# A two-layer feed-forward on one Trainium2 core: three quarters of the second matrix product by Strassen's seven block products

## The chip, the core and the metric

One core of one Trainium2 chip (trn2) runs the whole program. The metric is the device time of one execution in microseconds (us). Engines are named as in the profile: PE is TensorE's matmul stream, PEld its weight loads, DVE is VectorE, ACT is ScalarE, POOL is GpSimd, SP is SyncE, whose queue issues the weight transfers. Each engine runs its own instructions in a fixed order, written when the program is compiled, and the engines meet through semaphores.

## The reference, cut to what matters

The model is three blocks on 512 tokens of width 1024, all in float32. The change is in the feed-forward that ends each of the two layers of the second block:

```python
def squared_relu_mlp(n, w_up, w_down):          # n: 512 x 1024
    return jnp.square(jax.nn.relu(n @ w_up)) @ w_down   # w_up 1024 x 4096, w_down 4096 x 1024

for layer in range(DEPTH_2):                    # DEPTH_2 = 2
    n = rmsnorm_2(h, g_mix[layer])
    h = h + mixer(n, ...)                       # sparse attention + gated linear attention, then stick-breaking attention
    h = h + squared_relu_mlp(rmsnorm_2(h, g_ffn[layer]), w_up[layer], w_down[layer])
```

## The kernel before, in words

Activations stand feature-major: `x` is a list of eight tiles of 128 features by 512 tokens. A float32 product is made of three matmuls in the type fp32r: each operand is split into a rounded `hi` and a rest `lo`, and hi·hi, hi·lo and lo·hi are added up in PSUM. ACT writes `hi` (L148 for activations, L170 for weights), DVE writes `lo` (L149, L171).

- `proj_fm` (feature-major) loads 256 columns of a weight matrix in one transfer of 1 MB into `raw` (two buffers), splits them in two halves of 128 columns into `whi` and `wlo` (three buffers each, L170 and L171), and calls `fm_tile` for each half: 8 blocks of the contraction times three matmuls (L246 to L248), 24 matmuls with 512 moving columns and 128x128 weights, into one PSUM bank of the tag `mm` (four banks). Then `evac` takes the bank.
- `proj_tok` (token-major) does the same with the activations as weights and 512 columns of the weight matrix moving (L282 to L284), four banks at a time.
- `first()` raises the priority of what is traced in it, so that the compiler's scheduler places splits and evictions early in their engines' queues. Within that the scheduler orders instructions by when their inputs and buffers are ready.
- `mlp_up` (L1098) makes one quarter of the hidden features, 1024 of 4096: eight `fm_tile`s, each taken by DVE (`ha`, L1107: relu times the norm's scale), squared on ACT (L1108) and split again (L148, L149).
- The feed-forward of layer 0 loops over four quarters `g`: `mlp_up`, then `proj_fm` over the 1024 rows of `w_down0` that belong to the quarter; each of its eight tiles is added to `x` by DVE (`add_to`, L1075), the last quarter's by `residual` (L1066), which also splits for the next layer.
- The feed-forward of layer 1 does the same, but the second product is token-major: in quarter 0 the eight tiles of `x` are transposed by PE (L331) and copied by ACT (L1240) to `xo`, and every quarter adds to `xo` on DVE (L1245); the last quarter sends `xo` out.
- Every slot of 128x512 float32 comes from a tag with a fixed number of buffers (`SLOTS`): `s` 39, `o` 8, `go` 6, `isc` 3, `att` 4, `Ss` 4, `pTs` 2, `g` 4, `sq` 2. `kz` are the keys of an early attention, padded with zeros by POOL (L400).

Of the kernel before, what the change touches and what calls it, by code (L numbers as in the profile page):

```python
# [8 lines left out]
F32 = mybir.dt.float32  # L9
# [25 lines left out]

SLOTS = {"s": 39, "x": 8, "o": 8, "att": 4, "isc": 3, "go": 6, "Ss": 4, "pTs": 2, "g": 4, "sq": 2}

FILL = 480  # L40
BANKS = {"mm": 4, "S0": 1, "S1": 1, "pT": 1, "acc": 1}


def body(tc, A, out, dbg=None):
# [3 lines left out]
    with ExitStack() as es:  # L48
# [26 lines left out]
        def first():  # L75

            return tc.high_priority(3000)
# [28 lines left out]
            o, w = CV[name]  # L106
            return vec[:, o:o + w]

        ident = cp.tile([P, P], F32, name="ident")
# [77 lines left out]
        def later(f):  # L187
            pending.append(f)
# [35 lines left out]
        def drain(gen):  # L224
            for _ in gen:
                pass
# [27 lines left out]
        def proj_fm(W, r0, c0, ncols, xs, evac):  # L254


            kd = len(xs)
            w = 1024 // kd
            for ch in range(0, ncols, 2 * w):
                cw = min(2 * w, ncols - ch)  # L260
                raw = load_raw(kd, cw, (0, W[r0:r0 + kd * P, c0 + ch:c0 + ch + cw]))
                for hf in range(0, cw, w):
                    hi, lo = split_w(raw[:, :, hf:hf + w], w)
                    for mt in range(0, w, P):
                        fm_tile(hi, lo, mt, xs, evac, (ch + hf + mt) // P)
                        yield
# [158 lines left out]
        with tc.issue_after(box["v"].ins):  # L425
            gab = cp.tile([P, 3 * P], F32, name="gab")
            nc.scalar.dma_start(gab, A["gab"])
            ropeA = cp.tile([P, NT, 2, 32], F32, name="ropeA")
            nc.scalar.dma_start(ropeA, A["ropeA"])
            ropeI = cp.tile([P, NT, 2, 16], F32, name="ropeI")  # L430
# [12 lines left out]
            NRB = rb.shape[1]  # L443
            bias = []
            for h2 in range(4):
                rv = slot("biasr", tag="g")
                for j in range(2):
                    h = 2 * h2 + j
                    nc.scalar.dma_start(rv[:, j * 256:(j + 1) * 256],
                                        bass.AP(tensor=rb.tensor, offset=rb.offset + h * NRB, ap=[[1, P], [1, 256]]))  # L450
                b = slot("bias", tag="go")
                DVE.tensor_copy(heads(b, 2), heads(rv, 2)[:, :, ::-1])
                for j in range(2):
                    DVE.memset(b[0:64, j * 256 + 192:(j + 1) * 256], NEG)
                    bias.append(b[:, j * 256:(j + 1) * 256])
# [290 lines left out]
        drain(proj_fm(W, 0, 2376, 256, nx, ev_kb))  # L746


        n0 = cp.tile([P, P], F32, name="negm0")
        POOL.memset(n0, 0.0)  # L750
        POOL.memset(n0[0:64, 64:128], NEG)
        negm = [n0]
# [345 lines left out]
        dump("x3", x)  # L1098


        def mlp_up(Wu, g, nxs, rbc):
            hid = [None] * KD

            def ev(i, ps):
                def f():
                    a = slot("ha", tag="g")
                    DVE.scalar_tensor_tensor(a, ps, 0.0, box[rbc], op0=ALU.max, op1=ALU.mult)  # L1107
                    ACT.activation(a, a, AF.Square)  # L1108
                    hid[i] = split(a, tag="o" if i < 4 else "s")
                if rbc in box:  # L1110
                    f()
                else:
                    later(f)

            drain(proj_fm(Wu, 0, g * 1024, 1024, nxs, ev))
            return hid

        nx4 = [None] * KD
        T4 = cp.tile([P, NT], F32, name="T4")
        t4sq = cp.tile([P, NT], F32, name="t4sq")  # L1120
        for g in range(4):
            hid = mlp_up(A["w_up0"], g, nx3, "t3b")
            if g == 3:
                ss4 = SumSq()
            drain(proj_fm(A["w_down0"], g * 1024, 0, 1024, hid,
                          add_to(x) if g < 3 else residual(x, ss4, "gm1", nx4, lambda: (
                              scale_of(ss4, T4)(), DVE.tensor_tensor(t4sq, T4, T4, op=ALU.mult)))))
        dump("x4", x)


# [98 lines left out]


        xo = []
        for g in range(4):
            hid = mlp_up(A["w_up1"], g, nx5, "t5b")
            if g == 0:
                for tt in range(NT):
                    row = []
                    for hf in range(2):
                        ps = transposed([(j, blk(x[hf * 4 + j], tt)) for j in range(4)])
                        t_ = slot("xo", tag="go" if hf else "att")
                        ACT.activation(t_, ps, AF.Copy)  # L1240
                        row.append(t_)
                    xo.append(row)
            for hf in range(2):
                def ev_o(tt, ps, hf=hf, g=g):
                    DVE.tensor_tensor(xo[tt][hf], ps, xo[tt][hf], op=ALU.add)  # L1245
                    if g == 3:
                        nc.sync.dma_start(out[tt * P:(tt + 1) * P, hf * 512:(hf + 1) * 512], xo[tt][hf])

                drain(proj_tok(A["w_down1"], g * 1024, hf * 512, hid, ev_o))


def host_arrays(inp):
# [53 lines left out]
```

## Time and profile before

| | |
|---|---|
| three runs | 1654.59, 1658.58, 1658.85 us; median 1658.58 us |
| the profiled execution | 1655.4 us, of which the span from first to last instruction is 1653.7 us |
| mean granted TensorE clock | 0.99 of full speed |
| matmuls | 7576, each with its own weight load |
| the two feed-forwards | 16 stages of 1024x1024 weights by 512 tokens, 43.5 us each: 696 us |
| transfers | 146 MB, 88 GB/s over the span |

How it is read: an engine's busy time is the union of its instructions. Matmuls are pipelined, so that one lasts about 390 ns from start to end while the next starts much earlier; the pace of PE is the distance between starts, not the duration of one. "Idle before" is the time that an engine stood still ahead of an instruction, with what released it behind the arrow.

### The profile page before, as it was taken

To read this page: it belongs to the slowest core of one execution; us is meant where nothing else is said; L and a number is where in the kernel's file an instruction comes from. 1 tells how busy PE (TensorE), PEld (TensorE's weight loads), DVE (VectorE), ACT (ScalarE), POOL (GpSimd) and SP (SyncE) were. 2 spreads that over 40 slices of the span, in tenths; PEclk is the share of its full clock that TensorE was granted. 3 is DMA by queue.
4 is the path that set the end of the run, shared out by engine and by line. 5 is a ranking of instruction groups with operands and counts; after the bars stand their busy time and mean duration, and the time that the engine had idled before them with its cause. 6 is when DMAs were issued, how large, how long until landed. Compare 5 with 4: busy or idle time off the path is not lost.

```text
span 1653.7 us, 19122 instructions
## 1 busy us (share of the span) xinstructions
PE 1620.5 (98%) x7576; PEld 1331.8 (81%) x7576; DVE 847.7 (51%) x1463; ACT 653.3 (40%) x1012; POOL 208.8 (13%) x295
## 2 busy tenths in 40 slices
PE   9999999999898889999999999999999999999999
PEld 7887888888687768888888888888888788888887
DVE  5546443444668885654343444444557734444342
ACT  6444333235544445443232323344554532323231
POOL 3100000003412641210000000211212200000000
PEclk9999999999999999999999999999999999999999
DMA  6421123223212111133323232222211323332222
GB/s 203 148 76 52 52 85 118 89 98 109 94 60 77 52 52 52 52 102 102 100 82 99 102 102 100 80 100 77 77 52 52 102 77 102 102 102 85 94 102 77
DMA packets 123065, 146.25 MB, mean 88 GB/s; under 512 B 4048, under 2 KB 96864, under 8 KB 122976
## 3 DMA queue, kind: packets, MB, share of 16 engines
q1 hardware_dynamic: 116704, 141.11, 25.9%
q10 hardware_dynamic: 6272, 3.92, 0.9%
q8 instruction: 59, 0.97, 0.2%
q14 instruction: 30, 0.25, 0.0%
HBM read 142.92 MB, written 2.10 MB: 88 GB/s over the span
## 4 chain that ended last, share of the span: by engine, by line
PE 91%; DVE 4%; POOL 2%; ACT 1%; issue 1%; DMA 0%; POOLq 0%; DVEq 0%
PE fm L246 19%; PE fm L248 19%; PE fm L247 19%; PE tk L282 8%; PE tk L283 8%; PE tk L284 8%; PE tr L331 3%; PE oc L1201 1%; PE S L1177 1%; PE S L469 1%; PE pa L493 1%; DVE wlo L171 1%; DVE isc L786 1%; DVE m L785 1%; PE gr L887 1%
## 5 line engine op out<-in xcount | busy, mean ns | idle before, releaser
L246 PE MATMUL fm<-hi,whi 128*128 128x512 f32 x1416 | 559.2, 395 | 0.0
L247 PE MATMUL fm<-lo,whi 128*128 128x512 f32 x1416 | 552.5, 390 | 0.8 <-DVE lo L152 0.8
L248 PE MATMUL fm<-hi,wlo 128*128 128x512 f32 x1416 | 552.8, 390 | 0.0
L170 ACT ACTIVATE whi<-raw 128x1024 fp32r<-128x1024 f32 (+1 forms) x262 | 276.9, 1057 | 691.7 <-PE fm L247 460.5
L171 DVE TENSOR_TENSOR wlo<-raw,whi 128x1024 fp32r<-128x1024 f32 (+1 forms) x262 | 328.3, 1254 | 276.8 <-ACT whi L170 276.0
L247 PEld LDWEIGHTS fm<-lo,whi 128*128 128x128 f32 x1416 | 266.4, 188 | 55.7 <-DVE lo L152 2.0
L248 PEld LDWEIGHTS fm<-hi,wlo 128*128 128x128 f32 x1416 | 266.0, 188 | 55.7
L246 PEld LDWEIGHTS fm<-hi,whi 128*128 128x128 f32 x1416 | 266.1, 188 | 53.4 <-issue 0.5
L282 PE MATMUL tk<-whi,hi 128*128 128x512 f32 x664 | 270.5, 407 | 0.7 <-ACT va L795 0.6
L283 PE MATMUL tk<-wlo,hi 128*128 128x512 f32 x664 | 262.1, 395 | 0.0
L284 PE MATMUL tk<-whi,lo 128*128 128x512 f32 x664 | 261.6, 394 | 0.0
L284 PEld LDWEIGHTS tk<-whi,lo 128*128 128x128 f32 x664 | 125.8, 189 | 26.6
L282 PEld LDWEIGHTS tk<-whi,hi 128*128 128x128 f32 x664 | 126.4, 190 | 24.8 <-ACT va L795 1.0
L283 PEld LDWEIGHTS tk<-wlo,hi 128*128 128x128 f32 x664 | 126.2, 190 | 23.5 <-issue 0.4
L308 POOL TENSOR_TENSOR ssq<-ssq,sq 128x512 f32<-128x512 f32 x25 | 38.6, 1553 | 567.1 <-ACT sq L306 566.8
L1075 DVE TENSOR_TENSOR xT<-fm,xT 128x512 f32<-128x512 f32 x48 | 33.1, 690 | 87.4 <-PE fm L248 87.3
L1107 DVE SCALAR_TENSOR_TENSOR ha<-fm,t3b 128x512 f32<-128x512 f32 x32 | 22.0, 691 | 80.0 <-PE fm L248 80.0
L1107 DVE SCALAR_TENSOR_TENSOR ha<-fm,t5b 128x512 f32<-128x512 f32 x32 | 22.0, 691 | 79.4 <-PE fm L248 79.4
L149 DVE TENSOR_TENSOR lo<-ha,hi 128x512 fp32r<-128x512 f32 x64 | 44.3, 692 | 3.0 <-ACT hi L148 3.0
L148 ACT ACTIVATE hi<-ha 128x512 fp32r<-128x512 f32 x64 | 40.5, 633 | 2.0
L1108 ACT ACTIVATE ha<-ha 128x512 f32<-128x512 f32 x64 | 39.6, 618 | 2.8 <-DVE ha L1107 2.8
L1190 DVE TENSOR_TENSOR_SCAN R<-sgn,zero 128x128 f32<-128x128 f32 (+3 forms) x32 | 27.0, 843 | 21.1 <-POOL sgn L1184 21.1
(308 smaller groups left out, 1371.7 us busy)
## 6 DMA issues: line engine op xcount, KB each, us to landing
raw<-in_w_up SPq DMA_DIRECT2D x32, 1024.0 KB, 5.1
raw<-in_w_down SPq DMA_DIRECT2D x32, 1024.0 KB, 5.0
raw<-in_w_in SPq DMA_DIRECT2D x22, 1024.0 KB, 5.1
raw<-in_w_in_ab SPq DMA_DIRECT2D x14, 1024.0 KB, 4.8
raw<-in_w_in_c SPq DMA_DIRECT2D x12, 1024.0 KB, 5.0
raw<-in_w_out SPq DMA_DIRECT2D x4, 1024.0 KB, 4.7
raw<-in_w_out_ab SPq DMA_DIRECT2D x4, 1024.0 KB, 4.8
raw<-in_w_out_c SPq DMA_DIRECT2D x4, 1024.0 KB, 4.8
```

The costliest lines, as they stand in the source:

```text
L148: ACT.activation(hi[:, cols], src[:, cols], AF.Copy)
L149: DVE.tensor_tensor(lo[:, cols], src[:, cols], hi[:, cols].bitcast(F32), op=ALU.subtract)
L170: ACT.activation(hi[:, ks, :], raw[:, ks, :], AF.Copy)
L171: DVE.tensor_tensor(lo[:, ks, :], raw[:, ks, :], hi[:, ks, :].bitcast(F32), op=ALU.subtract)
L246: PE.matmul(ps, wh, xh, start=k == 0, stop=False)
L247: PE.matmul(ps, wh, xl, start=False, stop=False)
L248: last = PE.matmul(ps, wl, xh, start=False, stop=k == kd - 1)
L282: PE.matmul(ps, xh, hi[:, j, :], start=k == 0, stop=False)
L283: PE.matmul(ps, xh, lo[:, j, :], start=False, stop=False)
L284: last = PE.matmul(ps, xl, hi[:, j, :], start=False, stop=k == kd - 1)
L331: PE.transpose(ps[:, j * P:(j + 1) * P], s_, ident)
L1107: DVE.scalar_tensor_tensor(a, ps, 0.0, box[rbc], op0=ALU.max, op1=ALU.mult)
```

## The change

In both layers the quarters 0, 1 and 2 of the second product go by Strassen's scheme in its form with seven products and shared sums. A pair of output tiles (256 features, `mp` 0 to 3) and a pair of contraction blocks form 2x2 blocks of 128x128 weights; the tokens are halved, so that the activations form 2x2 blocks of 128x256. Seven block products take the place of eight, each over four pairs of contraction blocks and three fp32r terms: 84 matmuls with 256 moving columns for a pair of output tiles, where 48 with 512 columns stood.

- `weight_forms` makes, from one `raw` of 1024x256, the split pieces A11 and A12 (one split of 1024 elements a row), and S1, S2, A22, S4 and S3 (four sums on DVE and five splits of 512 elements a row). A11/A12 and S1/S2 go into two of the three `whi`/`wlo` buffers, the other three into `isc` (hi) and `att` (lo).
- `forms` makes the pieces of two hidden tiles: four half sums on DVE, one half split (B11), three whole splits.
- `down_pair` runs the seven products into four banks, two products in each. Products 1 and 5, and 6 and 4, are kept in `E` for all three quarters (in quarter 0 by ACT, then added to by DVE); the others are added to `x` by DVE at once. `settle` adds `E` to `x` after the third quarter, seven DVE instructions for a pair of tiles.
- `mlp` orders the work: the first 256 columns of the next quarter's up stage now run ahead of the current quarter's down stage. Quarter 3 stays as it was. The transposes of `x` in layer 1 move from quarter 0 to the end of quarter 3's up stage.
- Slots: `s` 38, `go` 8; `kz` moves into the tag `x`; `ident`, `ropeI` and `n0` move into the room of a fill tile that shrinks by as much.

```diff
-SLOTS = {"s": 39, "x": 8, "o": 8, "att": 4, "isc": 3, "go": 6, "Ss": 4, "pTs": 2, "g": 4, "sq": 2}
-FILL = 480
+SLOTS = {"s": 38, "x": 8, "o": 8, "att": 4, "isc": 3, "go": 8, "Ss": 4, "pTs": 2, "g": 4, "sq": 2}
+FILL = 96
...
-                t_ = kz[2 * i + j] = slot("kz")
+                t_ = kz[2 * i + j] = slot("kz", tag="x")
...
+        def forms(q, b1, b2, res):
+            tA, tB = slot("tA", tag="pTs"), slot("tB", tag="pTs")
+            DVE.tensor_tensor(half(tB, 0), half(b1, 0), half(b1, 1), op=ALU.subtract)
+            DVE.tensor_tensor(half(tA, 0), half(b2, 1), half(tB, 0), op=ALU.add)
+            DVE.tensor_tensor(half(tB, 1), half(b2, 0), half(tA, 0), op=ALU.subtract)
+            DVE.tensor_tensor(half(tA, 1), half(b1, 1), half(b2, 1), op=ALU.subtract)
+            if q % 2 == 0:
+                res["B11"] = slot("hi", F32R), slot("lo", F32R)
+            h_, l_ = (half(t_, q % 2) for t_ in res["B11"])
+            ACT.activation(h_, half(b1, 0), AF.Copy)
+            DVE.tensor_tensor(l_, half(b1, 0), h_.bitcast(F32), op=ALU.subtract)
+            out = {"B11": (h_, l_)}
+            for (n1, n2), (src, tag) in {("T1", "T4"): (tB, "s"), ("T2", "T3"): (tA, "s"),
+                                         ("B21", "B22"): (b2, "o")}.items():
+                sp_ = split(src, tag=tag)
...
+        def weight_forms(raw):
+            r = raw.rearrange("p (j a) (b c) -> p j a b c", a=2, b=2)
+            a11, a12, a21, a22 = (r[:, :, a, b, :] for b in range(2) for a in range(2))
...
+            def put(src, hi, lo):
+                ACT.activation(hi, src, AF.Copy)
+                DVE.tensor_tensor(lo, src, hi.bitcast(F32), op=ALU.subtract)
+            with first():
...
+                put(raw[:, :, 0:P], hi, lo)
...
+                S = {n_: tile4(slot("ws", tag="Ss")) for n_ in ("S1", "S2", "S4", "S3")}
...
+                DVE.tensor_tensor(S["S1"], a21, a22, op=ALU.add)
+                DVE.tensor_tensor(S["S2"], S["S1"], a11, op=ALU.add)
+                for i, n_ in enumerate(("S1", "S2")):
+                    put(S[n_], hi2[:, i], lo2[:, i])
...
+                DVE.tensor_tensor(S["S4"], S["S2"], a12, op=ALU.add)
+                DVE.tensor_tensor(S["S3"], a11, a21, op=ALU.add)
+                for n_, src in (("A22", a22), ("S4", S["S4"]), ("S3", S["S3"])):
+                    h_, l_ = tile4(slot("wh", F32R, "isc")), tile4(slot("wl", F32R, "att"))
+                    put(src, h_, l_)
...
+        def down_pair(Wd, g, mp, F, x, E):
+            raw = load_raw(KD, 2 * P, (0, Wd[g * 1024:(g + 1) * 1024, mp * 2 * P:(mp + 1) * 2 * P]))
+            w = weight_forms(raw)
+            banks = [psum("sw") for _ in range(4)]
+            plan = (("A11", "B11"), ("S1", "T1"), ("S2", "T2"), ("A22", "T4"), ("A12", "B21"), ("S4", "B22"), ("S3", "T3"))
+            for n, (wf, xf) in enumerate(plan):
+                ps = banks[n // 2]
+                for j in range(4):
...
+                    PE.matmul(half(ps, n % 2), wh, xh, start=j == 0, stop=False)
+                    PE.matmul(half(ps, n % 2), wh, xl, start=False, stop=False)
+                    last = PE.matmul(half(ps, n % 2), wl, xh, start=False, stop=j == 3)
...
+                if n in (1, 3):
+                    if g == 0:
+                        E[mp][i] = slot("e", tag="go")
+                        ACT.activation(E[mp][i], ps, AF.Copy)
+                    else:
+                        DVE.tensor_tensor(E[mp][i], ps, E[mp][i], op=ALU.add)
+                elif n == 5:
+                    DVE.tensor_tensor(xa, ps, xa, op=ALU.add)
+                elif n == 6:
+                    DVE.tensor_tensor(heads(xb, 2), half(ps, 0)[:, None, :].to_broadcast([P, 2, H]), heads(xb, 2), op=ALU.add)
...
+            for g in range(4):
+                e_ = ev(g)
+                if g == 0:
+                    drain(proj_fm(Wu, 0, 0, 1024, nxs, e_))
+                else:
+                    if g < 3:
+                        forms(0, has.pop((g, 0)), has.pop((g, 1)), F)
+                    else:
+                        for mp in range(4):
+                            settle(mp, x, E)
+                    drain(proj_fm(Wu, 0, g * 1024 + 256, 768, nxs, lambda i, ps: e_(i + 2, ps)))
+                if g < 3:
+                    nxt = ev(g + 1)
+                    drain(proj_fm(Wu, 0, (g + 1) * 1024, 256, nxs, nxt))
+                    for mp in range(4):
+                        down_pair(Wd, g, mp, F, x, E)
+            return hid
...
-        for g in range(4):
-            hid = mlp_up(A["w_up1"], g, nx5, "t5b")
-            if g == 0:
-                for tt in range(NT):
...
+        hid = mlp(A["w_up1"], A["w_down1"], nx5, "t5b", x)
+        for tt in range(NT):
```

## Rows read from the trace of the kernel before

**Rows 1.** The page's first part: busy us, share of the span, instructions

```profile
PE 1620.5 (98%) x7576; PEld 1331.8 (81%) x7576; DVE 847.7 (51%) x1463; ACT 653.3 (40%) x1012; POOL 208.8 (13%) x295
```

**Rows 2.** The page's chain that ended last, shares of the span

```profile
PE 91%; DVE 4%; POOL 2%; ACT 1%; issue 1%; DMA 0%; POOLq 0%; DVEq 0%
```

**Rows 3.** Windows by stage: length, busy us of PE, PEld, DVE, ACT, POOL

```profile
804.38:847.90 43.52, 43.52 (x193) 36.04 (x192) 19.91 (x24) 16.59 (x23) 0.00 (x0) 1.00 0.31 99
847.90:891.42 43.52, 43.52 (x193) 36.04 (x192) 15.98 (x18) 9.65 (x11) 0.00 (x0) 1.00 0.30 94
...
1519.38:1562.90 43.52, 43.52 (x193) 36.04 (x192) 15.92 (x17) 9.42 (x10) 0.00 (x0) 1.00 0.30 94
```

**Rows 4.** Groups by shape, 715 to 1070 us: busy, mean ns, idle before

```profile
L246 PE MATMUL fm<-hi,whi 128*128 128x512 f32 x513 | 199.8, 389 | 0.0
...
L247 PEld LDWEIGHTS fm<-lo,whi 128*128 128x128 f32 x513 | 96.3, 188 | 20.1
```

**Rows 5.** PE's timeline at 475 us: start us, duration us

```profile
475.04 0.28 PE L157 MATMUL is<-hi,hi 128*128 128x256 f32 x1
475.16 0.28 PE L158 MATMUL is<-lo,hi 128*128 128x256 f32 x1
475.27 0.28 PE L159 MATMUL is<-hi,lo 128*128 128x256 f32 x1
475.39 0.40 PE L282 MATMUL tk<-whi,hi 128*128 128x512 f32 x1
475.63 0.40 PE L283 MATMUL tk<-wlo,hi 128*128 128x512 f32 x1
475.87 0.39 PE L284 MATMUL tk<-whi,lo 128*128 128x512 f32 x1
476.09 0.28 PE L157 MATMUL is<-hi,hi 128*128 128x256 f32 x1
```

**Rows 6.** The same view, eight matmuls of one column

```profile
1301.67 1.05 PE L315 MATMUL st<-ones,ssq 128*128 128x1 f32 x8
```

**Rows 7.** Groups by shape, DVE, whole span

```profile
L171 DVE TENSOR_TENSOR wlo<-raw,whi 128x1024 fp32r<-128x1024 f32 x260 | 327.0, 1258 | 276.5 <-ACT whi L170 275.8
L149 DVE TENSOR_TENSOR lo<-ha,hi 128x512 fp32r<-128x512 f32 x64 | 44.3, 692 | 3.0 <-ACT hi L148 3.0
L1075 DVE TENSOR_TENSOR xT<-fm,xT 128x512 f32<-128x512 f32 x48 | 33.1, 690 | 87.4 <-PE fm L248 87.3
...
L1192 DVE TENSOR_TENSOR sgp<-sgp,R 128x256 f32<-128x256 f32 x8 | 3.4, 424 | 0.9
```

**Rows 8.** DVE's timeline from 1519 us: start us, duration us

```profile
1519.38 0.69 DVE L1107 SCALAR_TENSOR_TENSOR ha<-fm,t5b 128x512 f32<-128x512 f32 x1 [2.69 <-PE fm L248]
1520.25 1.23 DVE L171 TENSOR_TENSOR wlo<-raw,whi 128x1024 fp32r<-128x1024 f32 x1 [0.18 <-ACT whi L170]
1521.44 0.69 DVE L149 TENSOR_TENSOR lo<-ha,hi 128x512 fp32r<-128x512 f32 x1
...
1539.10 2.73 DVE L1245 TENSOR_TENSOR xo<-tk,xo 128x512 f32<-128x512 f32 x4 [1.08 <-PE tk L284]
```

**Rows 9.** Groups by shape, ACT, whole span

```profile
L170 ACT ACTIVATE whi<-raw 128x1024 fp32r<-128x1024 f32 x260 | 275.7, 1060 | 691.3 <-PE fm L247 460.5 <-PE tk L284 186.5 <-issue 39.4
L148 ACT ACTIVATE hi<-ha 128x512 fp32r<-128x512 f32 x64 | 40.5, 633 | 2.0
...
L341 ACT ACTIVATE pTs<-tr 128x256 f32<-128x256 f32 x16 | 6.1, 383 | 8.3 <-PE tr L331 8.3
...
L1240 ACT ACTIVATE xo<-tr 128x512 f32<-128x512 f32 x8 | 4.7, 592 | 3.8 <-PE tr L331 3.8
```

**Rows 10.** DMA issues: KB each, median us to landing

```profile
raw<-in_w_down SPq DMA_DIRECT2D x32, 1024.0 KB, 5.0
```

**Rows 11.** Groups by shape, PE, whole span: transposes

```profile
L331 PE MATMUL tr<-ident,xT 128*128 128x128 f32 x32 | 4.9, 276 | 0.0
```

**Rows 12.** Groups by shape, POOL, whole span

```profile
L400 POOL MEMSET kz<- 64x512 f32 x8 | 4.2, 521 | 0.4
```

More of the change, by code (lines that the diff above doesn't have):

```diff
@@ L1098, in body @@
         dump("x3", x)
-        def mlp_up(Wu, g, nxs, rbc):
-            hid = [None] * KD
[L1104 to L1111, printed above, removed]
-                else:
-                    later(f)
-            drain(proj_fm(Wu, 0, g * 1024, 1024, nxs, ev))
+        H = T // 2
@@ new lines, in half, with relu_sq, ready @@
+        def half(t_, j):
+            return t_[:, j * H:(j + 1) * H]
+        def relu_sq(ps, rbc, tag):
+            a = slot("ha", tag=tag)
+            DVE.scalar_tensor_tensor(a, ps, 0.0, box[rbc], op0=ALU.max, op1=ALU.mult)
+            ACT.activation(a, a, AF.Square)
+            return a
+        def ready(rbc, f):
+            if rbc in box:
+                f()
+            else:
+                later(f)
+        def forms(q, b1, b2, res):
[13 more added lines that the diff above has]
+                sp_ = split(src, tag=tag)
+                for j, n_ in enumerate((n1, n2)):
+                    out[n_] = tuple(half(t_, j) for t_ in sp_)
+            res[q] = out
@@ new lines, in weight_forms, with tile4 @@
+        def weight_forms(raw):
+            r = raw.rearrange("p (j a) (b c) -> p j a b c", a=2, b=2)
+            a11, a12, a21, a22 = (r[:, :, a, b, :] for b in range(2) for a in range(2))
+            res = {}
+            def tile4(t_):
+                return t_.rearrange("p (j c) -> p j c", j=4)
+            def put(src, hi, lo):
+                ACT.activation(hi, src, AF.Copy)
+                DVE.tensor_tensor(lo, src, hi.bitcast(F32), op=ALU.subtract)
+            with first():
+                hi = wp.tile([P, 8, P], F32R, tag="whi", bufs=3, name=uid("whi"))
+                lo = wp.tile([P, 8, P], F32R, tag="wlo", bufs=3, name=uid("wlo"))
+                put(raw[:, :, 0:P], hi, lo)
+                for a, n_ in enumerate(("A11", "A12")):
+                    res[n_] = [(hi[:, 2 * j + a, :], lo[:, 2 * j + a, :]) for j in range(4)]
+                S = {n_: tile4(slot("ws", tag="Ss")) for n_ in ("S1", "S2", "S4", "S3")}
+                hi2 = wp.tile([P, 2, 4, P], F32R, tag="whi", bufs=3, name=uid("whi"))
+                lo2 = wp.tile([P, 2, 4, P], F32R, tag="wlo", bufs=3, name=uid("wlo"))
+                DVE.tensor_tensor(S["S1"], a21, a22, op=ALU.add)
+                DVE.tensor_tensor(S["S2"], S["S1"], a11, op=ALU.add)
+                for i, n_ in enumerate(("S1", "S2")):
+                    put(S[n_], hi2[:, i], lo2[:, i])
+                    res[n_] = [(hi2[:, i, j, :], lo2[:, i, j, :]) for j in range(4)]
+                DVE.tensor_tensor(S["S4"], S["S2"], a12, op=ALU.add)
[3 more added lines that the diff above has]
+                    put(src, h_, l_)
+                    res[n_] = [(h_[:, j, :], l_[:, j, :]) for j in range(4)]
+            return res
@@ new lines, in settle, with both @@
+        def settle(mp, x, E):
+            e15, e64 = E[mp]
+            xa, xb = x[2 * mp], x[2 * mp + 1]
+            def both(t_):
+                return t_[:, None, :].to_broadcast([P, 2, H])
+            DVE.tensor_tensor(heads(xa, 2), heads(xa, 2), both(half(e15, 0)), op=ALU.add)
+            DVE.tensor_tensor(half(xa, 1), half(xa, 1), half(e64, 0), op=ALU.subtract)
+            DVE.tensor_tensor(half(xa, 1), half(xa, 1), half(e15, 1), op=ALU.add)
+            DVE.tensor_tensor(half(e64, 0), half(e64, 0), half(e15, 0), op=ALU.subtract)
+            DVE.tensor_tensor(heads(xb, 2), heads(xb, 2), both(half(e64, 0)), op=ALU.add)
+            DVE.tensor_tensor(half(xb, 0), half(xb, 0), half(e64, 1), op=ALU.add)
+            DVE.tensor_tensor(half(xb, 1), half(xb, 1), half(e15, 1), op=ALU.subtract)
@@ new lines, in mlp, with ev, f_, f @@
+        def mlp(Wu, Wd, nxs, rbc, x):
+            hid = [None] * KD
+            E = [[None, None] for _ in range(4)]
+            has, F = {}, {}
+            def ev(g):
+                def f_(i, ps):
+                    def f():
+                        if g < 3:
+                            has[g, i] = relu_sq(ps, rbc, "sq" if g and i < 2 else "g")
+                            if i % 2 and not (g and i == 1):
+                                forms(i // 2, has.pop((g, i - 1)), has.pop((g, i)), F)
+                        else:
+                            hid[i] = split(relu_sq(ps, rbc, "g"), tag="o" if i < 4 else "s")
+                    ready(rbc, f)
+                return f_
+            for g in range(4):
+                e_ = ev(g)
+                if g == 0:
+                    drain(proj_fm(Wu, 0, 0, 1024, nxs, e_))
+                else:
+                    if g < 3:
+                        forms(0, has.pop((g, 0)), has.pop((g, 1)), F)
+                    else:
+                        for mp in range(4):
+                            settle(mp, x, E)
+                    drain(proj_fm(Wu, 0, g * 1024 + 256, 768, nxs, lambda i, ps: e_(i + 2, ps)))
+                if g < 3:
+                    nxt = ev(g + 1)
+                    drain(proj_fm(Wu, 0, (g + 1) * 1024, 256, nxs, nxt))
+                    for mp in range(4):
+                        down_pair(Wd, g, mp, F, x, E)
@@ L1120, in body @@
         t4sq = cp.tile([P, NT], F32, name="t4sq")
-        for g in range(4):
[L1122 to L1127, printed above, removed]
+        hid = mlp(A["w_up0"], A["w_down0"], nx3, "t3b", x)
+        ss4 = SumSq()
+        drain(proj_fm(A["w_down0"], 3072, 0, 1024, hid, residual(x, ss4, "gm1", nx4, lambda: (
+            scale_of(ss4, T4)(), DVE.tensor_tensor(t4sq, T4, T4, op=ALU.mult)))))
         dump("x4", x)
@@ L1231, in body, with ev_o @@
         xo = []
-        for g in range(4):
-            hid = mlp_up(A["w_up1"], g, nx5, "t5b")
-            if g == 0:
-                for tt in range(NT):
[L1236 to L1242, printed above, removed]
-            for hf in range(2):
[L1244 to L1249, printed above, removed]
+        hid = mlp(A["w_up1"], A["w_down1"], nx5, "t5b", x)
+        for tt in range(NT):
+            row = []
+            for hf in range(2):
+                ps = transposed([(j, blk(x[hf * 4 + j], tt)) for j in range(4)])
+                t_ = slot("xo", tag="go" if hf else "att")
+                ACT.activation(t_, ps, AF.Copy)
+                row.append(t_)
+            xo.append(row)
+        for hf in range(2):
+            def ev_o(tt, ps, hf=hf):
+                DVE.tensor_tensor(xo[tt][hf], ps, xo[tt][hf], op=ALU.add)
+                nc.sync.dma_start(out[tt * P:(tt + 1) * P, hf * 512:(hf + 1) * 512], xo[tt][hf])
+            drain(proj_tok(A["w_down1"], 3072, hf * 512, hid, ev_o))
 def host_arrays(inp):
```

11 lines of the change are left out of this document (8 added, 3 removed).

## The prediction

> **What bounds the kernel now.** I read the page's first part, its chain, and then the windows of the feed-forward stages. PE is busy 98% of the span, VectorE (DVE) 51% [rows 1], and PE carries 91% of the chain that ended last [rows 2]. [...] So here the time is the number of matmuls times their pace, 43.52/192 = 0.2267 us with 512 columns, and a tile of 24 takes 5.44 us. The duration of one, 389 ns [rows 4], is latency and says nothing of pace. DVE has 16.0 us of work in a down stage and ACT at most 9.7 [rows 3]: the room that the change wants to use.
>
> **Removed and added on PE.** The change touches 24 pairs of output tiles (2 layers x 3 quarters x 4). Each had 48 matmuls, 2 x 5.44 = 10.88 us, and gets 84 with 256 columns. Everything hangs on the pace of those. If it were half of 0.2267, 0.1133, a pair would take 9.52 us. The nearest rows are the score products of the early layer, fp32r, 256 columns, new weights each, three in a row [rows 5]: 475.04 to 475.39 is 0.35 us, 0.117 each. But the three matmuls of 512 columns behind them run slower than elsewhere: the six together take 1.05 us (475.04 to 476.09); less 3 x 0.2267 that leaves 0.37, 0.123 each. I take the middle, 0.120, and keep 0.1133 and 0.123 as ends. What could hold a long stream back is the weight load, one for each matmul; eight matmuls of one column, which can hardly be paced by anything else, follow each other at about (1.05 - 0.25)/7 = 0.114 us [rows 6], the last one's latency taken at about 0.25. That lies just under 0.120, so loads and columns cost nearly the same and I see no cliff. A pair: 84 x 0.120 = 10.08 us, 0.80 less than 10.88. Over 24 pairs: **19.2 us less on PE** (13.2 at 0.123, 32.6 at 0.1133).
>
> [...]
>
> **Added on DVE and ACT.** Back to back a DVE instruction of 512 elements a row costs 0.68 us (four in 2.73) and one of 1024 1.19 (1520.25 to 1521.44) [rows 8]; one of 256 0.42 [rows 7]. `weight_forms` for a pair: one split of 1024, four sums, five splits: 1.19 + 9 x 0.68 = 7.3 us on DVE. Taking the products out: 4 x 0.68 = 2.7 us (1.4 in quarter 0, where ACT does two). So DVE has 10.0 us for a pair in quarters 1 and 2, 8.7 in quarter 0, beside 10.08 on PE: the down stage comes out level between the two engines, where DVE had 16.0 of 43.5 before. ACT has 1.06 + 5 x 0.63 = 4.2 us a pair [rows 9] and stays beside it. `forms` for two hidden tiles: 5 x 0.42 + 3 x 0.68 = 4.1 us; a quarter's up stage then has 4 x 4.1 + 8 x 0.68 + 8 x 1.19 = 31 us of DVE in 43.5, covered.
>
> Does DVE hold for a whole down stage (4 x 10.08 = 40.3 us)? The 10.88 us of the next quarter's first two up tiles stand ahead of it. In them DVE must do the last `forms` (4.1), two `ha` (1.4), A11/A12 (1.2), S1 and S2 (1.4): 8.1 us, so the first product starts on time. If the rest of pair 0 (sums S4, S3, three splits: 3.4) slips into the stage, DVE has 3.4 + 3 x 7.3 + 4 x 2.7 + two splits for the next up tiles 2.4 = 38.5 us in 40.3. It fits, with little left.
>
> **What then waits.** The late pieces are S1 and S2: their `whi`/`wlo` buffer comes free when A12, the fifth of seven products, is done, and S1 is wanted after the next pair's first. That is three products, 4.3 us, for ACT 0.63, DVE 0.68 and a hand-over; between ACT and a waiting DVE 0.18 us pass today [rows 8]. Behind a DVE that stands waiting for this piece lie the evictions, which free the banks, and A22, S4, S3. I charge PE one exposed hand-over of 0.18 us a pair, 24 x 0.18 = **4.3 us**; the ends are 0, and, if all six hand-overs lie open in the level quarters, 16 pairs x (10.0 + 6 x 0.18 - 10.08) = 16 us.
>
> **What costs nothing, and its cover.** `settle`: 2 x 0.68 + 5 x 0.42 = 3.5 us a pair, 14 a layer, beside six up tiles of 32.6 us, in which DVE has 6 x (0.68 + 0.68 + 1.19) = 15.3; without that cover up to 14 us a layer. Transfers: SP still issues 1 MB for a pair, 5.0 us [rows 10], two buffers, one pair per 10 us, though `raw` is now held through the sums; an issue that waits for `raw` has only later weights queued behind it on SP. The moved transposes keep their 32 matmuls [rows 11] and eight ACT copies [rows 9]; today they run between matmuls with 0.0 idle, and quarter 3's products stand ready around them, but they now also wait for `settle`. Bounds 0 to 8 x 0.6 = 5 us, taken 0, since the row shows it. Padding `kz`, 8 x 0.52 us on POOL [rows 12], now waits for the end of the queries; the keys' first tile takes 5.44 us after that: 0. The addresses and the spare `go` slots: 0, nothing runs differently.
>
> **Sum.** 1655.4 (the profiled execution, span 1653.7) - 19.2 + 4.3 = 1640.5. The median of the runs is 3.2 us above the profiled execution, so I forecast 1643.7 us, rounded 1644.
>
> **Rivals.**
> 1. The seams take it all: 0.80 us of waits a pair, about four and a half of today's hand-overs, brings the time to 1655 to 1662. For it: DVE and PE level; buffers come free late. Against it: the queues are ordered by readiness, and the window is 4.3 us wide.
> 2. Slower, on DVE's queue. It is one fixed order. If the splits of S1 and S2 stand behind the nine other instructions that a pair has from the release on (6.1 us) and ACT's 0.63, the piece comes at 7.4 us instead of within 4.3 (0.68 of it the split itself), and PE waits some 3 us at that seam. At every second seam: 12 x 3 - 19.2 = +17, 1675 us; it decides from 0.80 us a pair on, about one such seam in four. For it: 38.5 of 40.3 us. Against it: at 51% busy such a pile has never shown in this trace, so nothing measures it.
> 3. The weight load paces the stream: a matmul waits for its load in full, 188 ns [rows 4]. A pair takes 84 x 0.188 = 15.8 us, +4.9 each, +118 in all: 1777 us. It decides from 10.88/84 = 0.1295 us on, 8% above my 0.120. The rows with three in a row speak against it, but no run of 84 is in the trace. [...]
>
> **How the numbers follow.** Forecast 0.65, rival 1 0.14, rival 2 0.16, rival 3 0.05. The forecast's own range is 1626 (0.1133, no wait) to about 1660 (0.123, all hand-overs). Below 1629 I leave 0.04, above 1670 about 0.13 (half of rival 2, rival 3). Range 1629 to 1670. A measurement of this kernel tells 0.3%, some 5 us, from no change. Faster takes the forecast and a little of rival 1's lower edge, less the forecast's own slow end: 0.65. Same: 0.15, most of rival 1. Slower: 0.20, rivals 2 and 3.
>
> **What would show it.** The distance between starts in a stream of 256-column matmuls: 0.120 (0.113 to 0.123) if the sum holds; 0.13 or more would make the prediction wrong at its first step. PE's idle time before the seven products: about 4 us, most of it released by the lo split of S1. A down stage of about 41 us in place of 43.5. DVE's busy time in it: 36 us or more. `settle` inside the last up stage with no idle PE behind it, and the transposes with none before them.

## The result and the profile after

The changed kernel takes 1640.67 us (median of 4 runs, 1639.93 to 1641.13); the kernel before, beside it, 1658.71 (1654.59 to 1659.31). The ratio is 0.9896, 95% interval [0.9879, 0.9913]: 18.0 us or 1.1% faster. The forecast was 1644. The profiled execution of after took 1639.93 us, its span is 1638.2 us; before it was 1655.4 and 1653.7, so between the two profiles lie 15.5 us.

The page's first part and chain of after, which answer to [rows 1, 2]:

```profile
PE 1601.4 (98%) x8440; PEld 1358.3 (83%) x8440; DVE 1040.7 (64%) x1887; ACT 732.9 (45%) x1172; POOL 207.8 (13%) x295
...
PE 90%; DVE 4%; POOL 2%; ACT 1%; issue 1%; DMA 0%; POOLq 0%; DVEq 0%
```

PE is still busy 98% of the span, but the span is shorter; 864 matmuls more are issued (8440 for 7576) and 19 us less of PE work is left. VectorE (DVE) went from 51% to 64%. In the chain PE still has 90%, and each of the three lines of the seven products (`sw`) has 5% of the span in it.

The windows by stage of after (length, busy us and instructions of PE, PEld, DVE, ACT and POOL, granted clock): the down stages of quarters 0, 1 and 2 in layer 0, and between the first two the up stage of 8 tiles:

```profile
775.01:815.33 40.32, 40.32 (x338) 40.28 (x337) 28.81 (x43) 22.26 (x33) 0.00 (x0) 1.00 0.30 93
815.33:858.87 43.54, 43.54 (x195) 36.07 (x194) 31.87 (x54) 20.31 (x31) 0.00 (x0) 1.00 0.33 108
858.87:899.18 40.31, 40.31 (x337) 40.27 (x336) 33.42 (x51) 17.82 (x25) 0.00 (x0) 1.00 0.29 93
942.73:983.04 40.31, 40.31 (x337) 40.27 (x336) 37.55 (x61) 17.09 (x24) 0.00 (x0) 1.00 0.30 92
```

A down stage takes 40.3 us where it took 43.52 [rows 3]. PE is busy through all of it, at a granted clock of 1.00, the same as before. PEld's busy time fills the stage too, 40.28 us for 36.04 before: weight loads now follow each other with no gap. VectorE has 28.8, 33.4 and 37.6 us of work where it had 16.0. One group of the products' matmuls, with its idle time in the last column:

```profile
L1193 PE MATMUL sw<-hi,whi 128*128 128x256 f32 x384 | 108.6, 283 | 0.0
```

That 0.0, which the page gives for the other groups of `sw` too, is the finding for the feed-forward: in 24 pairs PE waited for nothing. Six stages, each 43.52 - 40.31 = 3.2 us shorter, give **19.3 us**; the forecast was 19.2. The end of one stage on PE's timeline (start, duration): starts are 0.12 us apart, then the matmuls of 512 columns follow at 0.23 to 0.24.

```profile
899.07 0.28 PE L1194 MATMUL sw<-lo,wh 128*128 128x256 f32 x1
899.18 0.28 PE L1195 MATMUL sw<-hi,wl 128*128 128x256 f32 x1
899.30 0.40 PE L246 MATMUL fm<-hi,whi 128*128 128x512 f32 x1
899.54 0.40 PE L247 MATMUL fm<-lo,whi 128*128 128x512 f32 x1
```

So 19.3 us came (19.1 from the broadcast below to the end: 907.07 us for 926.14), and the profiles differ by only 15.5. The rest was lost before the feed-forward began. The broadcast of `T3`, the scale of the first feed-forward, is an instruction of PE that both kernels run just ahead of it: of before, and then of after.

```profile
727.55 0.60 PE L322 MATMUL bc<-ident,T 128*128 128x128 f32 x4
```

```profile
731.15 0.60 PE L322 MATMUL bc<-ident,T 128*128 128x128 f32 x4
```

Up to this point the change has only moved buffers, and the changed kernel is 3.6 us late. At the first product `S` of the sparse attention PE is 0.26 us behind before (596.44 us for 596.18); from there to about 625 us, in the sparse attention and the gated linear attention, it falls 3.6 us behind, and stays there. 19.1 - 3.6 = 15.5.

### The profile page after: what moved, and what is told of

It is laid out like the page before. It is cut to its first block, busy times and chain, and to the rows that moved or that the text cites. A ratio compares the mean times of both kernels' runs of the same rounds, so it can differ in the third digit from the quotient of the medians.

```text
span 1638.2 us, 21483 instructions
## 1 busy us (share of the span) xinstructions
PE 1601.4 (98%) x8440; PEld 1358.3 (83%) x8440; DVE 1040.7 (64%) x1887; ACT 732.9 (45%) x1172; POOL 207.8 (13%) x295
## 4 chain that ended last, share of the span: by engine, by line
PE 90%; DVE 4%; POOL 2%; ACT 1%; issue 1%; DMA 0%; POOLq 0%; DVEq 0%
PE fm L246 16%; PE fm L248 16%; PE fm L247 16%; PE tk L282 5%; PE tk L283 5%; PE tk L284 5%; PE sw L1195 5%; PE sw L1194 5%; PE sw L1193 5%; PE tr L331 3%; PE oc L1342 1%; PE S L1318 1%; PE S L469 1%; PE pa L493 1%; DVE wlo L171 1%
## 5 line engine op out<-in xcount | busy, mean ns | idle before, releaser
L246 PE MATMUL fm<-hi,whi 128*128 128x512 f32 x1224 | 484.2, 396 | 0.0
L247 PE MATMUL fm<-lo,whi 128*128 128x512 f32 x1224 | 477.5, 390 | 0.7 <-DVE lo L152 0.7
L248 PE MATMUL fm<-hi,wlo 128*128 128x512 f32 x1224 | 477.7, 390 | 0.0
L283 PE MATMUL tk<-wlo,hi 128*128 128x512 f32 x472 | 186.8, 396 | 0.0
L1195 PE MATMUL sw<-hi,wlo 128*128 128x256 f32 x384 | 108.7, 283 | 0.0
L1194 PE MATMUL sw<-lo,whi 128*128 128x256 f32 x384 | 108.7, 283 | 0.0
L1193 PE MATMUL sw<-hi,whi 128*128 128x256 f32 x384 | 108.6, 283 | 0.0
L283 PEld LDWEIGHTS tk<-wlo,hi 128*128 128x128 f32 x472 | 90.6, 192 | 15.5 <-DVE wlo L171 0.2
L1193 PE MATMUL sw<-hi,wh 128*128 128x256 f32 x288 | 81.5, 283 | 0.0
L1194 PE MATMUL sw<-lo,wh 128*128 128x256 f32 x288 | 81.5, 283 | 0.0
L1195 PE MATMUL sw<-hi,wl 128*128 128x256 f32 x288 | 81.5, 283 | 0.0
```

Source lines behind the costliest of these rows:

```text
L246: PE.matmul(ps, wh, xh, start=k == 0, stop=False)
L247: PE.matmul(ps, wh, xl, start=False, stop=False)
L248: last = PE.matmul(ps, wl, xh, start=False, stop=k == kd - 1)
L283: PE.matmul(ps, xh, lo[:, j, :], start=False, stop=False)
L1193: PE.matmul(half(ps, n % 2), wh, xh, start=j == 0, stop=False)
L1194: PE.matmul(half(ps, n % 2), wh, xl, start=False, stop=False)
```

## Where the 3.6 us went

PE loses them in two places. The first is the group of eight gram matmuls (L887), which waits for VectorE's maximum (L982): 2.08 us before, 4.84 after. PE's timelines of before, and then of after:

```profile
603.70 2.04 PE L887 MATMUL gr<-yz,dl 128*128 128x128 f32 x8 [2.08 <-DVE m L982]
```

```profile
602.44 2.04 PE L887 MATMUL gr<-yz,dl 128*128 128x128 f32 x8 [4.84 <-DVE m L982]
```

In after this group stands in PE's queue ahead of an `S` product of 256 columns and seven matmuls of 512, which before ran first. So PE waits with nothing to do, and that work comes behind the wait. From the first `S` product at 596 us to the first L957, 20.56 us pass for 19.24.

The second place is a later `S` product, of 384 columns. It waits for `gatt` (L892), which VectorE writes, in after alone; from the first L957 to it, 7.73 us pass for 5.68. Of before, and then of after:

```profile
621.10 0.89 PE L979 MATMUL S<-kaT,qaT 128*128 128x384 f32 x2
```

```profile
624.73 0.88 PE L979 MATMUL S<-kaT,qaT 128*128 128x384 f32 x2 [1.76 <-DVE gatt L892]
```

0.26 + 1.32 + 2.05 = 3.63. What makes VectorE late at the second place is one instruction ahead of `gatt`, L990, the scaling of the sparse attention's softmax, in place. VectorE's timeline of after has two long instances, of 1.27 and 1.71 us:

```profile
612.68 1.27 DVE L990 TENSOR_SCALAR S<-S,rc 128x384 f32<-128x384 f32 x1
...
622.20 1.71 DVE L990 TENSOR_SCALAR S<-S,rc 128x256 f32<-128x256 f32 x1
623.83 0.75 DVE L892 COPY_PREDICATED gatt<-gmask,gr 128x256 f32<-128x256 uint8 x2
```

The same two of before take 0.42 and 0.35 us. There it is L881, behind `gatt`, that is long (0.42 us is usual):

```profile
612.48 0.42 DVE L990 TENSOR_SCALAR S<-S,rc 128x384 f32<-128x384 f32 x1
...
619.74 0.35 DVE L990 TENSOR_SCALAR S<-S,rc 128x256 f32<-128x256 f32 x1
620.18 0.77 DVE L892 COPY_PREDICATED gatt<-gmask,gr 128x256 f32<-128x256 uint8 x2
620.99 1.26 DVE L881 TENSOR_TENSOR yz<-dl,qb 64x256 f32<-64x256 f32 x1
```

And POOL's timeline of after. The two long instances of L990 start at 612.68 and 622.20, the one together with a POOL instruction and the other within one that a second follows, and end 0.2 us after POOL's (613.73 and 623.76):

```profile
612.69 1.04 POOL L875 TENSOR_TENSOR dl<-Bc 128x512 f32<-128x512 f32 x1
...
622.02 0.73 POOL L881 TENSOR_TENSOR yz<-dl,qb 64x256 f32<-64x256 f32 x1 [2.71 <-PE gr L887]
622.72 1.04 POOL L875 TENSOR_TENSOR dl<-Bc 128x512 f32<-128x512 f32 x1
```

So the two instances take 0.85 and 1.36 us more than in before, and end about 0.2 us after POOL's instruction does, as if they waited for it; by what mechanism isn't shown, and that POOL holds them up is so far the author's reading of two meetings. The following experiments ask which part of the 3.6 us these meetings are, and what in the change brings the rest about.

**The allocation alone.** The first kernel is the one before with only the buffers changed:

```diff
-SLOTS = {"s": 39, ... "go": 6, ...}
+SLOTS = {"s": 38, ... "go": 8, ...}     # with kz in x, ident, ropeI and n0 moved, FILL = 96
```

> The kernel before with the change's allocation alone: s 38, go 8, kz in the tag x, ident, ropeI and n0 in the room of the fill tile; the feed-forward as before. The 3.6 us by which the changed kernel is late when it reaches the feed-forward stand between 527 and 622 us, in the sparse attention and the gated linear attention. Theory (the two spare go slots let the scheduler write another order there): +3.6 us on before, 1662 us, with PE's wait for the maximum of L982 ahead of a gram matmul at about 4.8 us in place of 2.1. Rival (the delay comes from the feed-forward's own code or from its transfers): 1658 to 1659 us, no change.

Measured: 1659.40 us, ratio to before 1.0012 [1.0002, 1.0023]; the broadcast of `T3` starts at 730.95 us in its profile, 3.4 us late, and PE has after's order with the gram wait of 4.85 us, as the theory said. So the feed-forward's code is not needed for the delay. By the ratio the kernel is 2.0 us above what before took beside it, by the medians 3.4; before's own runs lie in two groups, as told below, and all ten of this kernel, from 1658.1 to 1660.6, lie where the upper one does.

```diff
-"go": 8
+"go": 6
```

> As e1_slots, but go stays at 6: s 38, kz in x, ident, ropeI and n0 moved. Theory (the go slots): as before, 1658.7 us. Rival (the keys' new place, waiting for the queries' end, or s 38): +3.6 us, 1662 us, as e1_slots.

Measured: 1658.29 us, ratio 1.0009 [0.9998, 1.0019], and the broadcast at 732.11 us: late too, with PE's instructions in the very order of before and a gram wait of 2.23 us. The theory of the spare `go` slots expected no delay in this profile, and falls as the sole cause. L990 has two long instances, of 1.81 us at 605.57, which is another one than in after, and of 1.70 us at 623.20, which is the same.

The kernel before itself, in 19 runs beside these, took 1654.0 to 1656.0 us ten times and 1657.3 to 1660.3 nine times. Its profile, on which the prediction was made, is one of the first group, without a long L990. So it is likely that a long L990 befalls the kernel before in about half of its runs; no execution of its upper group was profiled, so this isn't shown.

**The changed kernel with go at 6.**

```diff
-"go": 8
+"go": 6, "ge": 2
-                        E[mp][i] = slot("e", tag="go")
+                        E[mp][i] = slot("e", tag="ge" if mp == 3 else "go")
```

> The changed kernel with go back at 6 and the last pair's two shared sums E in two slots of a tag of their own (ge). Theory (the go slots): the mixer's order of before comes back and the 3.6 us with it: 1640.7 - 3.6 = 1637 us, ratio 0.987. Rival (something else of the change delays the mixer): 1640.7 us.

Measured: 1640.48 us, ratio 0.9897 [0.9879, 0.9915], the same as after; the theory's 1637 did not come. Its profile is a lucky one (1638.34 us), with PE's order of before and one long L990 in place of two, at 620.49, and there PE reaches the broadcast 1.7 us earlier than in after:

```profile
729.41 0.60 PE L322 MATMUL bc<-ident,T 128*128 128x128 f32 x4
```

**The scaling on ACT**, which takes away what collides: the instruction leaves VectorE.

```diff
-DVE.tensor_scalar(s[:, :kmax], s[:, :kmax], rc, None, op0=ALU.mult)
+ACT.activation(s[:, :kmax], s[:, :kmax], AF.Copy, scale=rc)
```

> The changed kernel with the softmax scaling of the sparse attention (L990, a VectorE instruction with one SBUF input, in place) done by ACT; the sums are the same. In five profiles some of its 16 instances last 1.3 to 1.8 us where the shape's usual time is 0.28 to 0.42, each time with a POOL instruction under way, and the mixer is 2 to 5 us late behind them; in the profile of before none does. Theory (those collisions of VectorE and POOL are the 3.6 us by which the changed kernel's profile reaches the feed-forward late): no such instance is left, the feed-forward begins about 3 us earlier, 1637 to 1638 us. Rival (the delay has another cause, or the wait moves to another VectorE instruction): 1640 to 1641 us.

> The kernel before with the same scaling on ACT. Theory (whether the scaling collides with POOL makes the two groups of times of this kernel, 1654 to 1656 and 1657 to 1660 us, in 19 runs): all runs lie in the lower group, within 2 us, median 1655. Rival: both groups stay.

Measured: the changed kernel 1637.88 us (1637.60 to 1638.19), ratio 0.9883 [0.9863, 0.9904]; all of its runs lie below all runs of after. The feed-forward begins 2.1 us earlier than in after, and 1.5 us later than in before, since the gram wait is still 4.84 us:

```profile
729.07 0.60 PE L322 MATMUL bc<-ident,T 128*128 128x128 f32 x4
```

The kernel before with the same edit: 1656.41 us (1655.20 to 1658.57), ratio 1.0002 [0.9992, 1.0011]. Nine of its ten runs lie from 1655.2 to 1657.0 and one at 1658.6, where the unedited kernel beside it had four of thirteen above 1659. The upper group is thinned, not proven gone; the 2 us within which all runs were expected did not hold, and the median gains nothing. In its profiled execution the broadcast comes 0.2 us earlier than in before's, though ACT's scaling is no faster than an undisturbed one on VectorE (0.73 us for 512 elements, for 0.48); but from the last matmul to the end 5.49 us pass for 4.17, which stays unexplained. For the changed kernel the meetings of L990 with POOL account for 2.0 us between the profiled executions (1639.93 - 1637.91) and 2.8 between the medians (1640.67 - 1637.88), which were not taken beside each other.

**Both edits together.**

> The changed kernel with both edits: go at 6 with a tag of its own for two of the shared sums (e3_own), and the scaling on ACT (e9_act). Theory (the mixer's delay is made by collisions of VectorE and POOL, and the order of before has fewer of the others too): the feed-forward begins near 727.3 us as in e10_act_before, 1.7 us before e9_act, 1636 us. Rival (the order written with go at 8 costs nothing by itself): 1637.9 us as e9_act.

Measured: 1636.57 us (1635.60 to 1637.35), ratio 0.9877 [0.9860, 0.9894], beside 1657.87 for before: the fastest of all. PE reaches the broadcast at

```profile
726.82 0.60 PE L322 MATMUL bc<-ident,T 128*128 128x128 f32 x4
```

which is 0.7 us earlier than before did. So with the scaling off VectorE the order written with `go` at 6 is worth a further 1.3 us by the medians and 2.2 in the profiles. Of these 2.2, 1.7 lie in the stretch with the gram wait, which is 2.24 us for 4.84, and 0.6 ahead of it; that the order has fewer other meetings of VectorE and POOL, as the theory had it, isn't shown.

The traces side by side, in us (the five kernels of the next two sections, all with after's order and L990 on VectorE, have 7.73 or 7.74 in the fourth column):

| profile | gram wait | first `S` at 596 to first L957 | first L957 to `S` of 384 columns | long L990 | broadcast |
|---|---|---|---|---|---|
| before | 2.08 | 19.24 | 5.68 | none | 727.55 |
| after | 4.84 | 20.56 | 7.73 | 612.68, 622.20 | 731.15 |
| allocation alone, `go` 8 | 4.85 | 20.42 | 7.73 | 612.48, 622.00 | 730.95 |
| allocation alone, `go` 6 | 2.23 | 21.15 | 7.73 | 605.57, 623.20 | 732.11 |
| after, `go` 6 | 2.11 | 19.24 | 7.72 | 620.49 | 729.41 |
| after, scaling on ACT | 4.84 | 20.55 | 5.73 | on ACT | 729.07 |
| before, scaling on ACT | 2.24 | 18.89 | 5.50 | on ACT | 727.31 |
| after, both edits | 2.24 | 18.89 | 5.73 | on ACT | 726.82 |

Every trace with a long L990 between 620 and 624 us loses 2.0 us there, and none without it does. The one at 605.57 costs 1.9 us (21.15 for 19.24), the one at 612.68 nothing: 20.56 us with it, 20.55 without. When after's scaling is on ACT, L881 becomes long (1.20 and 1.24 us), as it is in before, so the meetings go on; what counts is whether the instruction that meets POOL stands ahead of a piece that PE waits for.

## What sets the pace of 256 columns

The kernels of this section and the next were each run once; where they are compared with after, it is from the broadcast on, so that the delay ahead of it does not enter.

**Fewer columns, same loads.**

```diff
-                for j in range(4):
+                for c in range(2):
+                    o = half(ps, n % 2)[:, c * P:(c + 1) * P]
+                    for j in range(4):
...
+                        PE.matmul(o, wh, xh, start=j == 0, stop=False)
```

> The changed kernel with each matmul of 256 columns in the seven products cut in two of 128 columns, each with its own weight load: 168 for a pair of tiles in place of 84, the same sums. Theory (at 256 columns the weight load already sets the pace or nearly so): a load cannot be made faster by fewer columns, so the pace stays between 0.112 and 0.120 us and a pair takes 19 to 20 us, about 1640 + 24 x 9.5 = 1868 us. Rival (the columns set the pace): 0.06 us each, the time stays near 1640 us.

Measured: 1848.16 us. A stage of 672 matmuls takes 74.9 us, and the starts on PE's timeline lie 0.11 us apart:

```profile
790.00 0.27 PE L1195 MATMUL sw<-hi,wh 128*128 128x128 f32 x1
790.11 0.28 PE L1196 MATMUL sw<-lo,wh 128*128 128x128 f32 x1
790.23 0.28 PE L1197 MATMUL sw<-hi,wl 128*128 128x128 f32 x1
```

74.88/671 = 0.1116 us. Half the columns save 0.008 us of 0.120. The rival (0.06 us) is out: at 128 columns the pace is no longer the columns'.

**Shorter loads, same columns.**

```diff
+                    o = half(ps, n % 2)
...
-                    PE.matmul(half(ps, n % 2), wh, xl, start=False, stop=False)
+                    PE.matmul(o[0:64], wh[:, 0:64], xl, start=False, stop=False)
```

> The changed kernel with most of the seven products' weight loads cut to 64 of 128 columns (all but the first of the first contraction pair and the last of the last, in each product), the moving 256 columns as they were; the other 64 rows of these terms are left out of the result. Theory (at 256 columns it is the weight load that sets 0.120 us, since 128 columns still took 0.112): with half a load the pace falls to what the columns alone need, 0.107 to 0.113 us, in the stretches of short loads, and the time by 24 x 84 x 0.6 x 0.01 = some 10 us to about 1630 us. Rival (a fixed cost for each matmul beside the columns): 0.120 us stays, 1640 us.

Measured: 1631.39 us, in a kernel that leaves out half of the output rows of most terms, and from the broadcast to the end 10.1 us less than after (896.97 for 907.07). The duration of a load falls from 192 to 135 ns, and the matmuls follow at 0.11 to 0.12 us, 38.51/335 = 0.115 on average with the remaining full loads among them and 0.1144 in the stretches of short loads, a little above the 0.107 to 0.113 expected:

```profile
L1195 PEld LDWEIGHTS sw<-hi,whi 128*128 128x128 f32 x96 | 18.0, 188 | 0.2
...
L1198 PEld LDWEIGHTS sw<-lo,whi 128*64 128x64 f32 x384 | 51.9, 135 | 0.2
```

```profile
790.57 0.28 PE L1198 MATMUL sw<-lo,wh 128*64 128x256 f32 x1
790.69 0.28 PE L1199 MATMUL sw<-hi,wl 128*64 128x256 f32 x1
790.81 0.28 PE L1197 MATMUL sw<-hi,wh 128*64 128x256 f32 x1
790.92 0.28 PE L1198 MATMUL sw<-lo,wh 128*64 128x256 f32 x1
```

So neither resource alone gives 0.120. With short loads the pace falls to about what half of 0.2267 would be, 0.1133, with few columns it is 0.1116; with both full, each matmul costs 0.005 to 0.008 us more than with either cut. The fixed cost of the rival, which no shorter load could have lowered, is out at 256 columns. Whether the 0.1116 at 128 columns is the length of the load or a fixed cost of each load and matmul isn't shown: no run has both cut.

## How much room VectorE had

**Three and six more VectorE instructions for a pair.**

```diff
                     put(src, h_, l_)
+                    for _ in range(1):              # 2 in the second kernel
+                        DVE.tensor_tensor(l_, src, h_.bitcast(F32), op=ALU.subtract)
```

> The changed kernel with three more VectorE instructions of 512 elements for each pair of output tiles: the lo splits of A22, S4 and S3 are written twice. At 0.60 us back to back that is 1.8 us a pair, 7.2 us a down stage, where VectorE is busy 28.8, 33.4 and 37.6 of 40.3 us in quarters 0, 1 and 2. Theory (the down stage has 3 to 11 us of room on VectorE, and work for the next up stage can slip): quarters 0 and 1 stay at 40.3, quarter 2 grows by up to 4.5: 1640 to 1649 us. Rival (its queue is already late somewhere, and each instruction ahead of a piece that PE waits for counts in full): 24 x 1.8 = +43, 1683 us.

Measured: 1644.88 us, within the expected range; from the broadcast to the end 5.9 us more than after. Quarter 0 stays at 40.3 us, quarters 1 (expected to stay too) and 2 take 41.7 and 41.8, in which VectorE is busy 39.5 us (windows of layer 0, columns as above):

```profile
858.07:899.80 41.73, 40.65 (x337) 40.39 (x336) 39.57 (x62) 17.77 (x25) 0.00 (x0) 1.00 0.29 91
943.35:985.16 41.81, 40.66 (x337) 40.40 (x336) 39.51 (x63) 17.17 (x24) 0.00 (x0) 1.00 0.30 90
```

and this is what PE waited for (total us, times, longest):

```profile
PE sw L1195 <- DVE e L1205: 4.5, 4, 1.1
```

The first to come late is the eviction of `E` (L1205 here, L1203 in after), which frees the bank, not a split of S1 or S2. The rival's 43 us are out.

> As e6_dve3 with six more instructions for each pair, 3.6 us a pair, 14.4 a down stage: 43, 48 and 52 us of work on VectorE in quarters 0, 1 and 2. Theory: VectorE now paces the stages, by 3, 7.5 and 11.6 us, 2 x 22 = +44 at most, less what slips into the up stages: 1665 to 1684 us. Rival (PE does not wait for VectorE's queue, only for its last piece): under 1650 us.

Measured: 1693.52 us, 9.5 us beyond the upper end. Down stages take 47.7 to 50.7 us, of which VectorE is busy 42 to 47; PE waits for evictions, and its granted clock falls (quarters 0 and 1 of layer 1, windows with columns as above; the granted clock is the number behind POOL's, 0.93 for 1.00):

```profile
1374.00:1422.00 48.00, 42.18 (x338) 41.93 (x337) 42.14 (x67) 22.13 (x33) 0.00 (x0) 0.93 0.25 79
1465.00:1515.00 50.00, 44.24 (x341) 43.78 (x340) 46.36 (x74) 17.72 (x25) 0.00 (x0) 0.93 0.24 75
```

```profile
PE sw L1195 <- DVE e L1205: 25.3, 10, 3.3
```

In the six down stages 136 of the distances between starts are 0.21 us in place of 0.12; the stretch from 800 to 804 us, behind a wait of 5.8 us, has a granted clock of 0.50. An estimate from these: 136 x 0.093 = some 12.7 us of the loss is clock, which the expectation did not have.

**The cover ahead of the down stage taken away.**

```diff
-                    drain(proj_fm(Wu, 0, (g + 1) * 1024, 256, nxs, nxt))
                     for mp in range(4):
                         down_pair(Wd, g, mp, F, x, E)
+                    drain(proj_fm(Wu, 0, (g + 1) * 1024, 256, nxs, nxt))
```

> The changed kernel with the next quarter's first 256 up columns emitted behind the down stage, not ahead of it, so that the products follow the last up tile at once. Theory (the 10.9 us of cover are needed by about 8 us of VectorE work: the last forms, A11/A12, S1, S2): six waits of 5 to 8 us, +30 to +48, 1670 to 1688 us, PE waiting for lo splits at the head of each down stage. Rival (the scheduler puts other ready matmuls there anyway): within 5 us of 1640.

Measured: 1645.13 us; from the broadcast to the end 4.3 us more than after, in six stages of 40.6 to 41.2 us:

```profile
765.14:805.74 40.60, 40.58 (x337) 40.36 (x336) 29.13 (x43) 21.90 (x33) 0.00 (x0) 1.00 0.30 92
849.29:890.53 41.24, 40.80 (x337) 40.41 (x336) 33.93 (x51) 17.68 (x25) 0.00 (x0) 1.00 0.30 91
```

The theory's 30 to 48 us are out, and the rival's "within 5 us" holds from the broadcast on. PE's timeline shows the products directly behind the last up tile, at 0.12 us, with no matmul of another stage between. But the scheduler did put ready matmuls there, the products' own: 45 matmuls on pieces of `whi` and `wlo` run before the first on A22, where after has 36, so nine of A12's are drawn ahead, while VectorE still splits the sums of the last hidden tile (until 770.4 us). The first hitch, 0.3 us, comes behind 32 matmuls; quarters 1 and 2 lose 0.9 us each, 0.4 of it in a wait for the eviction of `E`.

## Why the prediction was right, point by point

- **Removed and added on PE: right.** 0.120 us was forecast as the middle between 0.117 and 0.123 [rows 5], and 0.120 is the mean over 2010 distances. That both readings, without and with the slower neighbours, bound it was good reading; that it lies in their middle was luck, for no row said so. Rival 3 (0.188) did not happen. The estimate from one-column matmuls, 0.114 [rows 6], was near the 0.1116 of 128 columns, but "no cliff" was luck as much as reading: 256 columns take only 0.008 us more than 128.
- **VectorE: mis-sized, on the safe side.** The sum took 0.68 us for 512 elements [rows 8] and for 256 the duration, 0.42 [rows 7]. Behind each other the new instructions cost 0.60 and 0.34. VectorE's timeline of after, part of a pair:

```profile
872.41 0.68 DVE L1203 TENSOR_TENSOR e<-sw,e 128x512 f32<-128x512 f32 x1
874.18 1.29 DVE L1157 TENSOR_TENSOR wlo<-ws,whi 128x512 fp32r<-128x512 f32 x2 [1.09 <-ACT whi L1156]
875.39 0.68 DVE L1168 TENSOR_TENSOR ws<-raw 128x512 f32<-128x512 f32 x1
875.99 0.69 DVE L1157 TENSOR_TENSOR wl<-raw,wh 128x512 fp32r<-128x512 f32 x1
876.59 0.69 DVE L1169 TENSOR_TENSOR ws<-ws,raw 128x512 f32<-128x512 f32 x1
877.20 0.68 DVE L1203 TENSOR_TENSOR e<-sw,e 128x512 f32<-128x512 f32 x1
877.80 1.22 DVE L1157 TENSOR_TENSOR wlo<-raw,whi 128x1024 fp32r<-128x1024 f32 x1
878.93 0.68 DVE L1157 TENSOR_TENSOR wl<-ws,wh 128x512 fp32r<-128x512 f32 x1
```

  13 instructions at 0.60 and one of 1.13 are 8.9 us a pair in quarters 1 and 2, not 10.0, and the stage is not level but has 3 to 11 us of room; of the 36 us or more that were to show it, quarter 2 alone has 37.6. What passes from ACT to a waiting VectorE is visible (874.18), and PE doesn't feel it.
- **The stall term: failed.** 4.3 us of exposed hand-overs were charged to PE, and 0.0 came. A hand-over delays VectorE, and VectorE had over 1 us a pair to spare (10.08 - 8.9); the sum treated it as PE's.
- **"The addresses and the spare `go` slots: 0": failed.** In the profiled execution 3.6 us were lost there: 1.3 in the gram wait, by the order that the scheduler writes with `go` at 8, 2.0 by one meeting of L990 with POOL, and 0.3 ahead of both. It nearly equals the 4.3 that did not come: 1655.4 - 19.3 + 3.6 = 1639.7, beside 1639.93 measured and 1640.5 forecast. The forecast of the profiled execution was close by luck, because two wrong terms cancelled.
- **From the profiled execution to the median: failed.** 3.2 us were added because before's median lay so far above its profile. That distance was before's two groups of runs, with the profile from the lower; after's median is 0.7 above its profile. This is most of the 3.3 us between 1644 and 1640.67.
- **Cover: too large a price.** 8.1 us of VectorE work were put into the 10.9 us ahead of a stage; without that cover 4.3 us are lost in all six stages together, where the scheduler drew nine matmuls of another product ahead. `settle` and the transposes were hidden, as forecast: PE's timeline of after has the first and last group of transposes with no idle time before them.

```profile
1586.90 0.60 PE L331 MATMUL tr<-ident,xT 128*128 128x128 f32 x4
...
1597.04 0.64 PE L331 MATMUL tr<-ident,xT 128*128 128x128 f32 x4
```

- **Rivals 1 and 2** did not happen. Rival 2's mechanism is real, and its point of decision lies where the added instructions put it: three more for a pair cost 1.4 to 1.5 us a stage in quarters 1 and 2, six more 7.4 to 10.4 in each. Its place was wrong: evictions come late first.

## What to carry to other kernels

When a product is cut into narrower matmuls, price them from rows in which loads and matmuls alternate, and take the slower neighbours into the price; here 128 columns took 0.1116 us where 256 took 0.120, so the cut to 128 gained next to nothing. A waiting engine's hand-over is a cost of that engine: charge it to PE only when that engine has no room left (PE waited 0.0 us with over 1 us a pair to spare on VectorE, and a stage took 1.4 to 1.5 us more in quarters 1 and 2 with three more instructions for a pair). And before a profile is taken as the base of a sum, see which group of the kernel's own runs it belongs to; a change that only moves buffers can change the order of an engine's queue, and with it the time of stages that it doesn't touch (the allocation alone put the broadcast 3.4 us later).

## What the runs showed of the hardware that was not expected

VectorE's scaling of 256 elements took 0.35 us alone and 1.71 with a POOL instruction under way; a long one cost PE 1.9 to 2.0 us where it stood ahead of a piece that PE waits for, and at 612.68 us nothing. With full loads and 256 columns a matmul took 0.120 us, with half the columns 0.1116, with half the load 0.1144: here both count. And in the stages of 48 and 50 us in which PE stood idle 5.8 us, the mean granted clock was 0.93, where it was 1.00 in stages with about 1.1 us of idle time; some 12.7 us of the loss, by the estimate above, came on top of the waits.
